# Weight blocks of a seven-product matrix multiplication: low parts by VectorE instead of by adding transfers, and four pieces of work moved in the order

## The chip, the cores and the metric

The kernel runs on one core of a Trainium2 chip. Times are device microseconds (us) of one execution; the time before is the median of three runs. The profile is of one further execution. TensorE (PE in the profile) multiplies, with its weight loads shown as PEld; VectorE is DVE, ScalarE ACT, GpSimd POOL, and SyncE (SP) only issues transfers. GpSimd issues transfers as well.

## The reference

One layer of a block: a short gated convolution, then a mixture of 16 experts of which each picks 256 of the 2048 tokens. All of it is in float32. What the change touches is the first product, `h @ w_in`, and the gates around the convolution:

```python
def dwconv_centred(x, w):                       # three taps along the tokens
    ...
def short_conv_mixer(h, w_in, conv_w, w_out):   # h: 2048 x 1024, w_in: 1024 x 3072
    gate_b, gate_c, v = jnp.split(h @ w_in, 3, axis=-1)
    return (gate_b * dwconv_centred(gate_c * v, conv_w)) @ w_out
    ...
m_l = (silu_c @ ada_w[i] + ada_b[i])[:, None, :]
sh1, sc1, g1, sh2, sc2, g2 = jnp.split(m_l, 6, axis=-1)
hl = modulate(rms_norm(lat, norm_g[i, 0]), sh1, sc1)
yl = short_conv_mixer(hl, sc_w_in[j], sc_conv[j], sc_w_out[j])
lat = lat + g1 * yl
hl2 = modulate(rms_norm(lat, norm_g[i, 1]), sh2, sc2)
lat = lat + g2 * expert_choice_ffn(hl2, moe_router[i], moe_w_gate[i], moe_w_up[i], moe_w_down[i])
```

## The kernel before, in words

**Split operands.** TensorE takes float32 operands in a rounded form, so every operand is held as a high part and a low part: ScalarE copies the value into the rounded form (high), VectorE subtracts that from the value (low). A product is three matmuls: high by high, low by high, high by low.

**Stages.** The 2048 tokens are four quarters of 512. Up to about 70 us the first quarter is normalised, turned and multiplied with two channel tiles of `w_in`; from 70 to 105 us the second quarter meets the same two tiles (`in_mm`, L507, called in the loop at L958 for `ct` 0 and 1, with eight pieces `k` each). From 105 to 592 us the other channel tiles follow, in **units** and **steps** (below). From 592 to 800 us comes `w_out` with the router, then a short search for the chosen tokens, and from about 840 us the experts.

**Units and steps.** A unit takes two tiles of 128 channels through 1024 tokens. Weights and tokens are each cut into 2 x 2 blocks, and the four results come out of seven block products where the plain way takes eight, with sums and differences of blocks as operands. There are 21 units: 20 of seven steps and one (unit 8, `PLAIN`) of eight plain steps, 148 steps in all. A step is twelve matmuls of 128x512 (`product`, L862). Units 0 to 8 work on the first half of the tokens, units 9 to 20 on the second.

**Weights.** A unit reads two pieces of `w_in`, `a` and `b`, of 512 KB, each in two halves. `make_block` (L829) makes the operand of one step. In its order 0 to 6 it takes half 0 of `a`; then `b0 + b1`, then that minus `a0`, both in place of `b0`; then half 1 of `a`; `b1 - b0` in place of `a0`; `a1 - b0` in place of `b0`; half 1 of `b`. VectorE makes these four sums (L840 to L846) at the start of the block that needs them, ScalarE copies the high part (L848). The low part is VectorE's subtraction (L855), but for blocks 0 and 6 (from unit 9 on also 3) it is a transfer: ScalarE writes the negated high part (L851) and GpSimd issues a transfer that reads the same weights from memory a second time and adds them on the way (L852). Three pieces have buffers; `piece_done` calls the load of the next one, on SyncE's queue.

**Order.** The order is written out by hand, engine by engine. At step n the program first makes the block of step n+3 (from unit 9 on, of step n+4), then what the table `later` holds for n, then the step's matmuls and the copy of its result. `at(n, f)` puts work into that table. Each engine runs its own list strictly in order.

**Banks.** A unit uses three banks of PSUM. Steps 0, 2, 4 and 6 add up in the first one, and ScalarE copies it out after each of them (L929), so step i+2 waits for the copy of step i. Steps 1 and 5 share the second, step 3 has the third; VectorE adds them to what was copied (L931 to L935).

**Behind a unit.** Two units of three hold `gate_c` and `v`. At the first step of the next unit VectorE multiplies them (L877) and ScalarE scales the result (L882); at the second step two more operations of VectorE (L886, L888) end the convolution. The third unit holds `gate_b`, with a product (L896) and a store.

**Operands made meanwhile.** The token sums of the first half are made by `first_sums` (L743) in the loop at L958, stored to memory and fetched again (`load_full`, `split_full`). Those of the second half are made in steps 4 to 41: the tokens are loaded (L408), normalised (`rstd_of` on ScalarE and GpSimd, then L417 on VectorE), turned by TensorE (L424) and stored, with sums (`save_sums`, `save_last`). From step 36 on, sums over `ada_w` (L562, L564) run on VectorE. Small tables are made in steps 4 to 43.

## Time and profile before

| | |
|---|---|
| median of three runs | 1920.81 us (1918.68 to 1926.13) |
| the profiled execution's own time | 1917.77 us |
| its span in the profile | 1916.0 us |
| TensorE busy | 1812.1 us, 95% of the span |
| VectorE busy | 1249.3 us, 65% |
| ScalarE busy | 951.2 us, 50% |
| GpSimd busy | 391.9 us, 20% |
| the steps (first matmul of L865 to the last) | 105.3 to 592.4 us |

A slice of the page's second part is 1916.0 / 40 = 47.9 us, so the steps lie in slices 3 to 13 of 40. The row PEclk gives the clock that TensorE was granted, in tenths; in the views by stretch it is a fraction. "[2.61 <-DMA sb" at the end of a row says that the engine was idle for 2.61 us and that the landing of a transfer into a tile named `sb` ended that. The tile `sb` is a block of weights, `raw` a piece of `w_in`, `tg` and `hl` are token operands, `pm` is a bank, `cx` and `cy` are the results of a unit, `xt` holds tokens and `pt` turned tokens, `aw` rows of `ada_w`, `fu` and `fy` fetched token sums.

### The profile page before, as it was taken

Reading aid. Unit: us, or ns where it says so; the run is one execution under the profiler, and the core shown is the slowest. Engines: PE = TensorE matmul, PEld = TensorE weight load, DVE = VectorE, ACT = ScalarE, POOL = GpSimd, SP = SyncE. Lnnn points to the kernel's source line nnn. Section 1 sums busy time; section 2 is a strip of 40 time slices with the busy share of each in tenths; the row PEclk is TensorE's granted clock in tenths of the full one; section 3 lists DMA queues with packets and bytes.
Section 4 is the critical chain, followed back from the end, with each engine's and each line's share of the span. In section 5 each row is a group of like instructions: output and inputs, shape, how many; then the busy total and the mean of one; then the engine's idle time right before and its main releaser. Section 6 shows DMA issues by size and latency. Waiting matters only on the chain.

```text
span 1916.0 us, 29497 instructions
## 1 busy us (share of the span) xinstructions
PE 1812.1 (95%) x11415; PEld 1600.4 (84%) x11415; DVE 1249.3 (65%) x1752; ACT 951.2 (50%) x1298; POOL 391.9 (20%) x552
## 2 busy tenths in 40 slices
PE   7977889999999999689999999999999999999997
PEld 6756667787788888479899999999999999999996
DVE  6554567666666667888667656665765666576653
ACT  5534434644444555557445444554545455445542
POOL 2223331233331222320021202102210211121002
PEclk9988999999999999889999999999999999999999
DMA  9474678777868899476687887878787878878774
GB/s 339 167 214 121 171 214 229 205 183 167 198 151 281 255 236 260 150 231 199 198 253 215 246 245 251 232 224 266 221 239 235 256 220 241 254 242 231 224 231 84
DMA packets 337229, 420.43 MB, mean 219 GB/s; under 512 B 104116, under 2 KB 201696, under 8 KB 337088
## 3 DMA queue, kind: packets, MB, share of 16 engines
q1 hardware_dynamic: 283632, 312.59, 53.4%
q0 software_dynamic: 53456, 105.96, 21.7%
q8 instruction: 89, 1.46, 0.3%
q14 instruction: 52, 0.43, 0.1%
HBM read 331.97 MB, written 63.98 MB: 207 GB/s over the span
## 4 chain that ended last, share of the span: by engine, by line
PE 71%; DVE 8%; DMA 7%; issue 6%; ACT 5%; POOL 2%; SPq 0%; POOLq 0%; DVEq 0%; ACTq 0%
PE pm L1587 12%; PE pm L1589 12%; PE pm L1591 11%; PE pm L1656 6%; PE pm L1654 6%; PE pm L1655 6%; PE pm L866 3%; PE pm L865 3%; PE pm L867 3%; DMA sb<-in_sc_w_in_dram 2%; PE pm L1116 2%; PE pm L1117 2%; PE pm L1119 2%; ACT sb L848 1%; DMA hl<-hl 1%
## 5 line engine op out<-in xcount | busy, mean ns | idle before, releaser
L248 DVE TENSOR_TENSOR ws<-raw,ws 128x1024 fp32r<-128x1024 f32 x390 | 463.5, 1221 | 272.7 <-ACT ws L238 272.7
L238 ACT ACTIVATE ws<-raw 128x1024 fp32r<-128x1024 f32 x390 | 394.2, 1052 | 408.9 <-PE pm L1591 325.0
L1587 PE MATMUL pm<-xT,ws 128*128 128x256 f32 x2048 | 568.3, 278 | 1.6 <-ACT xT L1566 1.6
L1589 PE MATMUL pm<-xT,ws 128*128 128x256 f32 x2048 | 567.0, 277 | 1.9 <-DVE xT L1567 1.8
L1591 PE MATMUL pm<-xT,ws 128*128 128x256 f32 x2048 | 566.6, 277 | 0.0
L1589 PEld LDWEIGHTS pm<-xT,ws 128*128 128x128 f32 x2048 | 385.4, 188 | 3.9 <-DVE xT L1567 2.1
L1587 PEld LDWEIGHTS pm<-xT,ws 128*128 128x128 f32 x2048 | 385.5, 188 | 3.2 <-ACT xT L1566 2.0
L1591 PEld LDWEIGHTS pm<-xT,ws 128*128 128x128 f32 x2048 | 385.3, 188 | 0.0
L1684 POOL DMA_INDIRECT out_dram<-ot,idx x30 | 104.9, 3498 | 587.3 <-DVE ot L1673 583.3
L865 PE MATMUL pm<-tg,sb 128*128 128x512 f32 x472 | 191.2, 405 | 13.4 <-ACT cx L929 11.8
L866 PE MATMUL pm<-tg,sb 128*128 128x512 f32 x472 | 189.4, 401 | 15.2 <-DMA sb<-in_sc_w_in_dram 14.9
L1656 PE MATMUL pm<-ws,hT 128*128 128x512 f32 x504 | 198.3, 394 | 0.0
L1654 PE MATMUL pm<-ws,hT 128*128 128x512 f32 x504 | 198.1, 393 | 0.0
L1655 PE MATMUL pm<-ws,hT 128*128 128x512 f32 x504 | 197.0, 391 | 0.0
L867 PE MATMUL pm<-tg,sb 128*128 128x512 f32 x472 | 187.9, 398 | 0.0
L848 ACT ACTIVATE sb<-raw 128x512 fp32r<-128x512 f32 x144 | 88.9, 625 | 125.9 <-DVE raw L840 47.2
L866 PEld LDWEIGHTS pm<-tg,sb 128*128 128x128 f32 x472 | 91.4, 194 | 38.5 <-DMA sb<-in_sc_w_in_dram 18.7
L855 DVE TENSOR_TENSOR sb<-raw,sb 128x512 fp32r<-128x512 f32 x92 | 63.6, 692 | 91.1 <-ACT sb L848 91.1
L865 PEld LDWEIGHTS pm<-tg,sb 128*128 128x128 f32 x472 | 91.2, 193 | 38.0 <-ACT cx L929 16.4
L1656 PEld LDWEIGHTS pm<-ws,hT 128*128 128x128 f32 x504 | 94.7, 188 | 20.0
L1655 PEld LDWEIGHTS pm<-ws,hT 128*128 128x128 f32 x504 | 94.7, 188 | 19.8
L1654 PEld LDWEIGHTS pm<-ws,hT 128*128 128x128 f32 x504 | 94.7, 188 | 18.7
(388 smaller groups left out, 2743.5 us busy)
## 6 DMA issues: line engine op xcount, KB each, us to landing
raw<-in_moe_w_down_dram SPq DMA_DIRECT2D x128, 512.0 KB, 4.6
raw<-in_moe_w_gate_dram SPq DMA_DIRECT2D x126, 512.0 KB, 4.8
raw<-in_moe_w_up_dram SPq DMA_DIRECT2D x126, 512.0 KB, 4.3
raw<-in_sc_w_in_dram SPq DMA_DIRECT2D x42, 512.0 KB, 4.8
xt<-in_x_dram SPq DMA_DIRECT2D x32, 512.0 KB, 7.6
aw<-in_ada_w_dram POOLq DMA_DIRECT2D x32, 512.0 KB, 5.1
sb<-in_sc_w_in_dram POOLq DMA_DIRECT2D x52, 256.0 KB, 5.4
fu<-fscr SPq DMA_DIRECT2D x23, 512.0 KB, 4.4
```

What stands on the lines that cost most here:

```text
L238: nc.scalar.activation(t[:, 0], raws[n_high], AF.Copy)
L248: (eng or nc.vector).tensor_sub(t[:, 1, ..., s], raw[..., s], t[:, 0, ..., s].bitcast(F32))
L848: nc.scalar.activation(t[:, 0], full, AF.Copy)
L865: nc.tensor.matmul(o, t[:, 0, j], r[:, 0], start=(first and j == 0), stop=False, skip_group_check=True)
L866: nc.tensor.matmul(o, t[:, 1, j], r[:, 0], start=False, stop=False, skip_group_check=True)
L867: nc.tensor.matmul(o, t[:, 0, j], r[:, 1], start=False, stop=end, skip_group_check=True)
L1587: nc.tensor.matmul(o, w[:, 0, j, c0], xT[:, 0, k], start=(k == 0 and f % 2 == 0), stop=False, skip_group_check=True)
L1589: nc.tensor.matmul(o, w[:, 0, j, c0], xT[:, 1, k], start=False, stop=False, skip_group_check=True)
L1591: nc.tensor.matmul(o, w[:, 1, j, c0], xT[:, 0, k], start=False, stop=(k == KD - 1), skip_group_check=True)
L1654: nc.tensor.matmul(ps[s], h, w[:, 0, j], start=(k == 0), stop=False)
L1655: nc.tensor.matmul(ps[s], h, w[:, 1, j], start=False, stop=False)
L1656: nc.tensor.matmul(ps[s], l, w[:, 0, j], start=False, stop=(k == KD - 1))
```

## The change

1. Every low part of a weight block is VectorE's subtraction. L851 and L852 are gone.
2. Each of the four weight sums is made at the end of the block before the one that uses it. The load after piece `a` is called at the end of block 4 instead of block 5.
3. VectorE's additions from the banks after steps 3, 4 and 5 stand in the list of the next step.
4. In the loop at L958, `load_other` and `first_sums` come three or four pieces earlier, so that all four are in the first of the two tiles; the split of the first token sum is a function of its own, and the fetches are called earlier.
5. The roots (`rstd_of`) of the third and fourth quarter stand two steps ahead of the normalisation that uses them. For the third quarter the roots are at steps 6 to 9 (with the normalisation at 7 to 10 before, now 8 to 11) and the turns at 13 to 16 (11 to 14 before); for the fourth the loads are at step 16 (15), the roots at 18 to 21 (18 to 21), the normalisation at 20 to 23 (18 to 21).
6. The turns of the fourth quarter (`save_other`) stand a step ahead of the sums that use them: turns at 24, 28, 32, 36 (23, 27, 31, 35), sums at 25, 29, 33, 37 (23, 27, 31, 35), the last difference at 27, 31, 35, 39 (25, 29, 33, 37).
7. One buffer of 4 KB goes from the tiles `wide` (six to five) to the tiles `hl` (18 to 19); of the output stage's token tiles every third is now one of the latter.

VectorE, blocks 0 to 4 of the first unit (the loop's last pieces and step 0), before:

```order
L797 TENSOR_TENSOR tg<-fu,tg 128x2x512 x2
L840 TENSOR_TENSOR raw<-raw 128x512
L855 TENSOR_TENSOR sb<-raw,sb 128x512
L797 TENSOR_TENSOR tg<-fu,tg 128x2x512
L842 TENSOR_TENSOR raw<-raw 128x512
L855 TENSOR_TENSOR sb<-raw,sb 128x512 x2
```

And in the changed kernel, where L849 is the low part, L855 to L861 are the four sums and L807 is the split of fetched token sums:

```order
L807 TENSOR_TENSOR tg<-fu,tg 128x2x512
L849 TENSOR_TENSOR sb<-raw,sb 128x512
L855 TENSOR_TENSOR raw<-raw 128x512
L807 TENSOR_TENSOR tg<-fu,tg 128x2x512
L849 TENSOR_TENSOR sb<-raw,sb 128x512
L857 TENSOR_TENSOR raw<-raw 128x512
L807 TENSOR_TENSOR tg<-fu,tg 128x2x512
L849 TENSOR_TENSOR sb<-raw,sb 128x512 x2
L859 TENSOR_TENSOR raw<-raw 128x512
```

Block 0 has a subtraction of its own now, and each sum stands behind a low part instead of ahead of one.

VectorE, the last two steps of unit 10 and the first two of unit 11, before (L935 is a bank addition, L877 the product of `gate_c` and `v`):

```order
L855 TENSOR_TENSOR sb<-raw,sb 128x512
L564 SCALAR_TENSOR_TENSOR acc<-aw,s_col,acc 128x1024
L935 TENSOR_TENSOR cx<-cx,pm 128x512
L844 TENSOR_TENSOR raw<-raw 128x512
L855 TENSOR_TENSOR sb<-raw,sb 128x512
L877 TENSOR_TENSOR cy<-cx,cy 128x1024
L846 TENSOR_TENSOR raw<-raw 128x512
L855 TENSOR_TENSOR sb<-raw,sb 128x512
```

The same place now (L881 is the product):

```order
L849 TENSOR_TENSOR sb<-raw,sb 128x512
L564 SCALAR_TENSOR_TENSOR acc<-aw,s_col,acc 128x1024
L935 TENSOR_TENSOR cy<-cy 128x512
L849 TENSOR_TENSOR sb<-raw,sb 128x512
L859 TENSOR_TENSOR raw<-raw 128x512
L935 TENSOR_TENSOR cx<-cx,pm 128x512
L849 TENSOR_TENSOR sb<-raw,sb 128x512
L861 TENSOR_TENSOR raw<-raw 128x512
L881 TENSOR_TENSOR cy<-cx,cy 128x1024
L849 TENSOR_TENSOR sb<-raw,sb 128x512
```

The bank addition (`cx<-cx,pm`) has moved behind the next step's low part, which is VectorE's now, and a weight sum (L861) stands between the last low part and the product.

ScalarE around steps 7 and 8, where the first convolution starts, before (L287 is the square of a root, L882 the scaling, L848 a high part):

```order
L848 ACTIVATE sb<-raw 128x512
L287 ACTIVATE junk,ss<-xt 128x1024
L882 ACTIVATE cx<-cy,v_col 128x1024
L929 ACTIVATE cx<-pm 128x512
L848 ACTIVATE sb<-raw 128x512
L287 ACTIVATE junk,ss<-xt 128x1024
```

And now (L886 is the scaling, L933 the copy of a bank):

```order
L287 ACTIVATE junk,ss<-xt 128x1024
L933 ACTIVATE cy<-pm 128x512
L848 ACTIVATE sb<-raw 128x512
L287 ACTIVATE junk,ss<-xt 128x1024
L886 ACTIVATE cx<-cy,v_col 128x1024
L933 ACTIVATE cx<-pm 128x512
```

The squares begin a step earlier; the one of step 7 still stands ahead of the scaling.

The diff, cut to its core:

```diff
@@ first_sums
-            t = wide("tsum", [P, 2, QT])
+            t = tsum[j] = wide("tsum", [P, 2, QT])
             nc.vector.tensor_sub(t[:, 0], f[:, 0], lo[:, 0])
-            t1 = home(0, T1, j)
-            nc.scalar.activation(t1[:, 0], t[:, 0], AF.Copy)
             nc.vector.tensor_sub(t[:, 1], f[:, 1], t[:, 0])
...
-            nc.vector.tensor_sub(t1[:, 1], t[:, 0], t1[:, 0].bitcast(F32))
...
+        def first_split(j):
+            t, t1 = tsum.pop(j), home(0, T1, j)
+            nc.scalar.activation(t1[:, 0], t[:, 0], AF.Copy)
+            nc.vector.tensor_sub(t1[:, 1], t[:, 0], t1[:, 0].bitcast(F32))
...
+        def rstd_to(q, b):
+            rstds[q, b] = rstd_of(xq[q][b], hl_tile([P, D], BF, "junk"))
...
+        def save_other(j):
             hi = hi_of[j] = hl_tile([P, 2, QT], F32, "fx")
             for h in range(2):
                 turn_x(3, j + 4 * h)
                 full_x(3, j + 4 * h, hi[:, h])
@@ make_block
-            if u != PLAIN:
-                if i == 1:
-                    nc.vector.tensor_add(full, full, raw_half(b, 1))
-                elif i == 2:
-                    nc.vector.tensor_sub(full, full, raw_half(a, 0))
-                elif i == 4:
-                    nc.vector.tensor_sub(full, raw_half(b, 1), raw_half(b, 0))
-                elif i == 5:
-                    nc.vector.tensor_sub(full, raw_half(a, 1), full)
-                    piece_done(a)
             nc.scalar.activation(t[:, 0], full, AF.Copy)
-            if u != PLAIN and i in ((0, 6) if u < PLAIN else (0, 3, 6)):
-                src, offset, ap, _ = pieces[p]
-                nc.scalar.activation(t[:, 1], t[:, 0].bitcast(F32), AF.Copy, scale=-1.0)
-                nc.gpsimd.dma_start(t[:, 1], dram(src, offset + h * (KD // 2) * ap[1][0], [ap[0], [ap[1][0], KD // 2], ap[2]]),
-                                    accum_op=ALU.add)
-            else:
-                nc.vector.tensor_sub(t[:, 1], full, t[:, 0].bitcast(F32))
+            nc.vector.tensor_sub(t[:, 1], full, t[:, 0].bitcast(F32))
...
+            if i == 0:
+                nc.vector.tensor_add(raw_half(b, 0), raw_half(b, 0), raw_half(b, 1))
+            elif i == 1:
+                nc.vector.tensor_sub(raw_half(b, 0), raw_half(b, 0), raw_half(a, 0))
+            elif i == 3:
+                nc.vector.tensor_sub(raw_half(a, 0), raw_half(b, 1), raw_half(b, 0))
+            elif i == 4:
+                nc.vector.tensor_sub(raw_half(b, 0), raw_half(a, 1), raw_half(b, 0))
+                piece_done(a)
@@ unit_step
-            if i == 3:
-                nc.vector.tensor_add(x[:, q0], x[:, q0], o)
-            elif i == 4:
-                nc.vector.tensor_add(y[:, q1], y[:, q1], y[:, q0])
-            elif i == 5:
-                nc.vector.tensor_add(x[:, q1], x[:, q1], o)
+            if i in (3, 4, 5):
+                at(n + 1, lambda: nc.vector.tensor_add(*((x[:, q0], x[:, q0], o), (y[:, q1], y[:, q1], y[:, q0]),
+                                                         (x[:, q1], x[:, q1], o))[i - 3]))
@@ the loop over k, first tile (ct == 0)
+                    if k < 2:
+                        load_other(0, k)
+                    if k in (2, 4, 5, 6):
+                        j = (2, 4, 5, 6).index(k)
                         first_sums(j)
...
@@ the table
-            at(7 + n, lambda b=n: norm_x(2, b, None, rstd_of(xq[2][b], hl_tile([P, D], BF, "junk"))))
-            at(11 + n, lambda j=n: save_full(j))
-            at(15, lambda b=n: load_x(3, b, b + 1))
-            at(18 + n, lambda b=n: norm_x(3, b, None, rstd_of(xq[3][b], hl_tile([P, D], BF, "junk"))))
-            at(21 + 4 * n, lambda j=n: load_other(1, j))
-            at(23 + 4 * n, lambda j=n: save_sums(j))
-            at(25 + 4 * n, lambda j=n: save_last(j))
+            at(6 + n, lambda b=n: rstd_to(2, b))
+            at(8 + n, lambda b=n: norm_x(2, b, None, rstds.pop((2, b))))
+            at(13 + n, lambda j=n: save_full(j))
+            at(16, lambda b=n: load_x(3, b, b + 1))
+            at(18 + n, lambda b=n: rstd_to(3, b))
+            at(20 + n, lambda b=n: norm_x(3, b, None, rstds.pop((3, b))))
+            at(22 + 4 * n, lambda j=n: load_other(1, j))
+            at(24 + 4 * n, lambda j=n: save_other(j))
+            at(25 + 4 * n, lambda j=n: save_sums(j))
+            at(27 + 4 * n, lambda j=n: save_last(j))
```

More of the change, by code (lines that the diff above doesn't have):

```diff
@@ L374, in hl_tile @@
         def hl_tile(shape, dt=F32R, name="hl"):
-            return mix.tile(shape, dt, name=name, tag="hl", bufs=18)
+            return mix.tile(shape, dt, name=name, tag="hl", bufs=19)
         def big_tile(shape, dt=F32R, name="ws"):
@@ L383, in wide @@
         def wide(name, shape=[P, 2 * QT + 4], dt=F32):
-            return cvp.tile(shape, dt, name=name, tag="wide", bufs=6)
+            return cvp.tile(shape, dt, name=name, tag="wide", bufs=5)
         def m2(name, n=QT, dt=F32):
@@ L766, in save_sums @@
                 full_x(3, j + 4 * h, hi[:, h])
+        def save_sums(j):
+            lo = lo_of[j] = rows_F.pop(j)
+            hi = hi_of[j]
             nc.gpsimd.dma_start(fscr[1][B22, j], hi[:, 1])
@@ L858, in make_block @@
                     piece_done(p)
+                return
+            if i == 0:
[7 more added lines that the diff above has]
+                piece_done(a)
             elif i == 6:
@@ L1091, in m2 @@
             return mixd.tile([P, n], dt, name=name, tag="m2", bufs=5)
+        n_xt = [0]
         def b4(name, shape=[P, D]):
-            if name == "xt":
-                return mixd.tile(shape, F32, name=name, tag="xt", bufs=3)
+            n_xt[0] += name == "xt"
+            if name == "xt" and n_xt[0] % 3:
+                return mixd.tile(shape, F32, name=name, tag="xt", bufs=2)
             return hl_tile(shape, F32, name)
```

34 lines of the change are left out of this document (15 added, 19 removed).

## The prediction, made before the change was run

> **What bounds the kernel now.** I read the page's slices first, then stretches along the steps, then TensorE's waits there.
>
> ```profile
> PE   7977889999999999689999999999999999999997
> PEclk9988999999999999889999999999999999999999
> ```
>
> TensorE is full except in the first six slices and around slice 17, the search, which the change does not touch. So the first third of the steps is where time can be had. The stretches are steps 0-20, 21-41, 42-55, 56-147, and steps 95-110 as a measure.
>
> ```profile
> core 0: us, PE busy (x) PEld busy (x) DVE busy (x) ACT busy (x) POOL busy (x), PEclk, DMA share, GB/s
> 105.30:202.10 96.80, 72.92 (x285) 56.62 (x284) 46.99 (x74) 43.23 (x70) 27.15 (x107) 0.86 0.54 148
> 202.10:285.70 83.60, 69.32 (x286) 54.60 (x285) 52.63 (x73) 34.53 (x59) 28.45 (x46) 0.92 0.69 201
> 285.70:329.70 44.00, 41.08 (x173) 31.95 (x172) 34.62 (x44) 21.32 (x35) 8.15 (x12) 1.00 0.75 208
> 329.70:592.40 262.70, 257.62 (x1118) 209.06 (x1117) 177.10 (x220) 131.60 (x215) 75.08 (x101) 1.00 0.78 192
> 442.90:486.40 43.50, 43.50 (x193) 36.03 (x192) 29.98 (x37) 21.04 (x35) 14.61 (x19) 1.00 0.77 181
> ```
>
> The measure: 16 steps in 43.5 us, 2.72 us each, at full clock. 148 steps make 402.6 us. The steps also hold eight groups of turns and eight sums of `ada_w`:
>
> ```profile
> 181.00 1.03 PE L424 MATMUL pt<-identf,xt 128*128 128x128 f32 x8
> L571 PE MATMUL pt<-acc,ones_f 128*128 128x512 f32 x16 | 7.6, 596 | 0.3 <-DVE acc L564 0.3
> ```
>
> At about 0.9 (the 1.03 overlaps its neighbour) and 7.6 in all, that is 7.2 + 7.6, and the floor is 417.4 us. The stage takes 592.4 - 105.3 = 487.1. The excess of 69.7 is waits, and matmuls at half clock.
>
> ```profile
> PE pm L866 <- DMA sb<-in_sc_w_in_dram: 21.1, 12, 4.8
> PE pm L865 <- ACT cx L929: 11.8, 7, 2.6
> PE pt L424 <- DVE xt L417: 11.0, 4, 4.1
> PE pm L865 <- ACT sb L848: 1.4, 1, 1.4
> ```
>
> These make 45.3 us (total, times, longest). Half clock costs 0.14 x 96.8 + 0.08 x 83.6 = 20.2. The remaining 4 are shorter waits and restarts. The first wait, in the timeline (start, duration, engine), shows all of it:
>
> ```profile
> 103.24 1.37 POOL L852 DMA_DIRECT2D sb<-in_sc_w_in_dram  x1 [0.55 <-ACT sb L851]
> 105.28 0.39 PE L865 MATMUL pm<-hl,sb 128*128 128x512 f32 x1
> 108.28 0.80 PE L866 MATMUL pm<-hl,sb 128*128 128x512 f32 x1 [2.61 <-DMA sb<-in_sc_w_in_dram]
> 108.87 0.63 PE L867 MATMUL pm<-hl,sb 128*128 128x512 f32 x1
> ```
>
> The transfer, issued at 103.24, lands 5 us later; TensorE idles 2.61 us and then takes 0.63 for a matmul instead of 0.39.
>
> The Trainium skill, "TensorE: Matmul & The Clock Gate", section "Part 1: The HAM clock gate (the "warmup" mystery)", halves the clock after an idle window of about 3.4 us. The trace differs: 2.61 was enough. By the rule the slow clock that I leave below (3.4 us) would be nothing and the time 1874; the row decides.
>
> **Low parts by VectorE.** Per block it removes 0.63 us of ScalarE, 1.37 of GpSimd and a landing, and adds one L855 to VectorE (groups by line: count, busy time, mean ns, idle time before):
>
> ```profile
> L851 ACT ACTIVATE sb<-sb 128x512 fp32r<-128x512 f32 x51 | 32.3, 633 | 1.6
> L852 POOL DMA_DIRECT2D sb<-in_sc_w_in_dram x51 | 67.9, 1367 | 127.3 <-ACT sb L851 126.2 <-issue 0.8
> L855 DVE TENSOR_TENSOR sb<-raw,sb 128x512 fp32r<-128x512 f32 x92 | 63.6, 692 | 91.1 <-ACT sb L848 91.1
> ```
>
> Steps 0-20 and 21-41 have six such blocks each, steps 42-55 four, the rest 36. VectorE's busy time becomes 47.0 + 4.2 = 51.2, 52.6 + 4.2 = 56.8, 34.6 + 2.8 = 37.4 and 177.1 + 24.9 = 202.0. The floors of these stretches are 60.7 (21 x 2.72 + 3.6), 60.7, 39.1 and 256. So it hides, but VectorE is at 94 and 96% in the second and third. The 21.1 us go whole.
>
> **Weight sums a block ahead.** No work is added. ScalarE's high part no longer waits for VectorE:
>
> ```profile
> L848 ACT ACTIVATE sb<-raw 128x512 fp32r<-128x512 f32 x143 | 88.3, 625 | 125.9 <-DVE raw L840 47.2 <-DVE raw L842 35.0 <-DVE raw L846 28.8
> L840 DVE TENSOR_TENSOR raw<-raw 128x512 f32<-128x512 f32 x20 | 13.7, 685 | 1.0 <-DMA raw<-in_sc_w_in_dram 1.0
> ```
>
> That ends the 1.4 and the stalls of ScalarE behind which copies of banks were late. But it lengthens one chain. At a unit's first step VectorE's product and ScalarE's scaling stand ahead of the copy for which TensorE waits two steps on; unit 11 started at 393.5 (timeline):
>
> ```profile
> 393.70 0.60 ACT L929 ACTIVATE cy<-pm 128x512 f32<-128x512 f32 x1 [1.67 <-PE pm L867]
> 394.19 0.62 ACT L848 ACTIVATE sb<-raw 128x512 fp32r<-128x512 f32 x1
> 394.85 0.69 DVE L855 TENSOR_TENSOR sb<-raw,sb 128x512 fp32r<-128x512 f32 x1 [0.88 <-ACT sb L848]
> 395.46 1.22 DVE L877 TENSOR_TENSOR cy<-cx,cy 128x1024 f32<-128x1024 f32 x1
> 396.79 1.16 ACT L882 ACTIVATE cx<-cy,v_col 128x1025 f32<-128x1025 f32 x1 [1.98 <-DVE cy L877]
> 397.86 0.57 ACT L929 ACTIVATE cx<-pm 128x512 f32<-128x512 f32 x1
> 398.94 0.39 PE L865 MATMUL pm<-tg,sb 128*128 128x512 f32 x1
> ```
>
> The copy ended at 398.43, 0.5 ahead of its user at 398.94. A sum of 0.685 now stands between L855 and L877, so TensorE waits 0.2 at each of 14 units: **2.8 us**. Where VectorE comes late to that place, the lateness is added.
>
> ```profile
> L768 DVE TENSOR_TENSOR fy<-fx,fy 128x512 f32<-128x512 f32 x4 | 2.8, 693 | 6.9 <-ACT fx L715 6.9
> L888 DVE SCALAR_TENSOR_TENSOR cx<-cy,v_col,cx 128x1025 f32<-128x1025 f32 (+1 forms) x14 | 18.0, 1286 | 1.1
> L564 DVE SCALAR_TENSOR_TENSOR acc<-aw,s_col,acc 128x1024 f32<-128x1024 f32 x28 | 35.8, 1278 | 6.0 <-DMA aw<-in_ada_w_dram 6.0
> ```
>
> I keep a running balance of VectorE's list per step against 2.72 us, never under zero, in durations of these rows (L768 stands for a token sum or a bank addition, two L888 for the end of a convolution) and of L840, L855 and L877. Step 25 has a low part, a weight sum, a bank addition and four token sums, 4.8 us; step 29 is 6.7 (a low part, a weight sum, 2.57 and four token sums); 37 to 43 average 3.2 with an L564 in most. The balance is 0.6 at step 28, 1.9 at 35 and 3.0 at 49: **5.5 us**. It falls to zero between bursts from unit 9 on, except where an L564 meets the product (steps 92, 120, 134). There waits of 1.1 and 0.6 stand among the 11.8 now; each of three grows by 0.7: **3.7 us**.
>
> The balance peaks at 6.8, at step 43. A block has three steps, 8.2 us, less about 2 for copy, high and low part, so it comes 0.6 late there; L564's 6.0 us for its `aw` fall into the same stretch, and the bound is 0.6 to 6.6. I take **4 us**.
>
> **Bank additions a step back.** VectorE no longer waits for the end of the current step. The price is ScalarE's copy of step 6, which overwrites what step 4's addition reads; that addition ends 3.3 us after the start of step 5, 2.1 before the copy, so it costs nothing while the balance is under 2.1. At the peak it is in the 4 us.
>
> **Roots and turns.** The turns of step 11 waited for a chain of square, root and normalisation inside one step (timeline; the last row is a load's time to landing):
>
> ```profile
> 163.52 0.48 PE L424 MATMUL pt<-identf,xt 128*128 128x128 f32 x1 [4.14 <-DVE xt L417]
> 168.08 1.33 PE L424 MATMUL pt<-identf,xt 128*128 128x128 f32 x5 [4.08 <-DVE xt L417]
> 167.27 0.75 DVE L417 TENSOR_SCALAR xt<-xt,rstd 128x1024 f32<-128x1024 f32 x1 [3.81 <-POOL rstd L290]
> xt<-in_x_dram SPq DMA_DIRECT2D x8, 512.0 KB, 7.6
> ```
>
> Now two steps lie between, and the 8.2 us of the third quarter go. Its squares begin at step 6, after loads called at step 4 that take 7.6 to land: ScalarE stands about 2 us, and the scaling of step 7 has a square ahead of it: **2 us** at step 9. For the fourth quarter the last normalisation is one step ahead of the turn: it ends about 3.6 us after step 23 starts, against 2.72: **0.9 us**, where 2.8 stood.
>
> **Token sums of the first half.** They move into the first tile's 19 us (70 to 89), where VectorE has to do 20 us of work; it ends about 7 late, inside the second tile's 16 us. TensorE had no wait there. Their fetches are called 6 to 10 us sooner; one held ScalarE for 7.2 us in step 0, behind which the 1.4 and two L929 waits stand:
>
> ```profile
> L796 ACT ACTIVATE tg<-fu 128x1024 fp32r<-128x1024 f32 x15 | 15.7, 1045 | 7.2 <-DMA fu<-fscr 7.2
> ```
>
> I cost the move at nothing; without that cover block 0 is late, by up to 3 us.
>
> **Buffers.** Five `wide` tiles are as many as a group of three units holds, so the copy of a fourth unit's second result can wait for a product (L896, 1.2 us) with a step of 2.72 in between: nothing. The output stage had waits of under 2 us in 200 and keeps its three token tiles: nothing.
>
> **The sum.** After: 2.8 + 5.5 + 3.7 + 4 + 2 + 0.9 = 18.9 us of waits. Slow clock: I allow two windows of half clock, 3.4 us lost (the 2.61 us wait above cost some 2). Restarts and late landings that I can't see: 4, as now. Excess 26.3, stage 443.7, gain 69.7 - 26.3 = 43.4. The profiled execution's own time, 1917.8, becomes 1874.4. The median of the runs is 3.0 above that execution, so the forecast is **1877 us**.
>
> **Rivals.**
> - *VectorE becomes the bound*, in lockstep with ScalarE. For: 94 and 96% above, and L855 waits 0.99 us per block (91.1 / 92). If that is not hidden in steps 0-55, they take 51.2 + 56.8 + 37.4 + 56 x 0.99 = 200.8 against 224.4 now; with 1.5 from later steps the gain is 25: 1896. Against: a wait of VectorE is spare time while it is ahead, and goes when it is behind.
> - *Almost everything goes*: an excess of 8 us, 1859. For: the balance counts no slack in ScalarE. Against: L564 and its `aw`.
> - *Locked port.* GpSimd's copy ahead of L882 takes 0.63 us for two elements:
>
> ```profile
> L878 POOL COPY cy<-carry 128x2 f32<-128x2 f32 x14 | 8.7, 625 | 0.0
> ```
>
>   If VectorE's two-input work holds it up by one instruction more at 14 units, 9.7 us: 1887. The row alone speaks for it. The Trainium skill, "SBUF — State Buffer", section "SBUF: two separate sides", states such a lock between a VectorE operation with two SBUF inputs and a GpSimd one that reads SBUF; no run here shows it apart.
> - *Slower.* VectorE falls over 2.7 us behind at each unit's start, so each of 20 units loses the longest L929 wait, 2.6, and a half-clock window, 1.7: 86 us against 65.5 recovered (45.3 + 20.2): 1941. Against: 79% load from step 56 on.
> - *No change.* Pieces of weights, called 8.2 us before use, land in over 10 us, and some 30 of them are 2.2 late: 66 us, 1921. Against: L840 waited 1.0 us for `raw` in all.
>
> **Numbers.** Forecast 0.52 (own range 1865 to 1890), lockstep 0.20, almost everything 0.12, port 0.06, slower 0.05, no change 0.05. A measurement tells 0.5%, about 10 us, from no change. Faster 0.90, same 0.05, slower 0.05. The range of 1857 to 1901 holds the forecast, the port, most of lockstep, and the nearer part of almost everything.
>
> **What would show it.** Right: no wait of TensorE on a transfer in the steps; the clock at 0.97 or more from 105 to 300; L424's wait under 3 us; steps 0-55 in 175 to 190 us; a wait of 0.2 on L929 at most units. Wrong: VectorE near 100% in steps 21-55 with TensorE waiting for low parts (lockstep); GpSimd as ScalarE's releaser at the scaling (port); waits on `raw` (no change).

## The result, and the profile after

The changed kernel takes 1868.93 us (median of four runs, 1868.14 to 1870.37) against 1923.47 us of the kernel before (four runs, 1918.68 to 1927.15): a ratio of 0.9719, with a 95% interval of 0.9692 to 0.9745. The forecast was 1877 us with a range of 1857 to 1901. The profiled execution took 1868.36 us with a span of 1866.3, against 1917.8 and 1916.0 before.

First the page's slices of the kernel after:

```profile
PE   7999989999999999599999999999999999999997
PEclk9999999999999999799999999999999999999999
```

Slices 3 to 6 of TensorE's row, which stood at 7, 7, 8 and 8, are now 9, 9, 9 and 8, and the clock, at 8 in slices 3 and 4 before, stays at 9 up to the search. The stretches of the steps, in the columns of the same view of before (the whole stage, then steps 0-20, 21-41, 42-55 and 56-147):

```profile
105.24:543.20 437.96, 425.34 (x1858) 344.79 (x1857) 334.92 (x457) 194.23 (x323) 80.78 (x215) 0.99 0.54 172
105.24:168.60 63.36, 61.20 (x285) 50.52 (x284) 46.06 (x77) 38.15 (x64) 26.93 (x103) 1.00 0.52 175
168.60:231.30 62.70, 61.31 (x286) 50.55 (x285) 50.90 (x73) 28.77 (x49) 18.91 (x37) 1.00 0.65 216
231.30:280.20 48.90, 43.45 (x174) 33.46 (x173) 38.85 (x52) 19.85 (x32) 6.29 (x10) 0.93 0.61 200
280.20:543.20 263.00, 259.37 (x1118) 210.26 (x1117) 199.11 (x258) 107.45 (x179) 28.65 (x65) 0.99 0.50 156
```

The stage fell from 487.1 to 438.0 us: 49.1 of the span's 49.7 us are here. Over the floor of 417.4 us it has an excess of 20.6, where 69.7 stood and 26.3 was forecast. VectorE is busy in 73, 81, 79 and 76% of the four stretches. What TensorE still waits for in the stage (total, times, longest):

```profile
PE pm L869 <- ACT cx L933: 8.1, 5, 2.3
PE pt L571 <- DVE acc L564: 4.0, 1, 4.0
PE pt L424 <- DVE xt L417: 0.4, 1, 0.4
```

No wait on a transfer is left (21.1 us before), and the waits on the normalised tokens fell from 11.0 to 0.4. The longest wait is new, at the sum of `ada_w` for the searched router, before step 47. Two groups by line show the two halves of a block now (count, busy, mean ns, idle before):

```profile
L849 DVE TENSOR_TENSOR sb<-raw,sb 128x512 fp32r<-128x512 f32 x144 | 98.5, 688 | 85.8 <-ACT sb L848 85.4
L848 ACT ACTIVATE sb<-raw 128x512 fp32r<-128x512 f32 x144 | 88.6, 626 | 53.8 <-DVE raw L855 23.5
```

VectorE forms all 144 low parts, at 688 ns. ScalarE's idle time ahead of the high parts went from 125.9 to 53.8 us.

### The profile page after: what moved, and what is told of

Its sections match the earlier page's. It is cut to its first block, busy times and chain, and to the rows that moved or that the text cites. A ratio compares the mean times of both kernels' runs of the same rounds, so it can differ in the third digit from the quotient of the medians.

```text
span 1866.3 us, 29372 instructions
## 1 busy us (share of the span) xinstructions
PE 1798.3 (96%) x11415; PEld 1595.0 (85%) x11415; DVE 1276.3 (68%) x1804; ACT 916.9 (49%) x1246; POOL 333.1 (18%) x500
## 4 chain that ended last, share of the span: by engine, by line
PE 82%; DVE 6%; DMA 4%; issue 4%; ACT 3%; POOL 1%; POOLq 0%; SPq 0%; ACTq 0%; DVEq 0%
PE pm L1595 12%; PE pm L1597 12%; PE pm L1599 12%; PE pm L1664 6%; PE pm L1662 6%; PE pm L1663 6%; PE pm L869 5%; PE pm L870 5%; PE pm L871 5%; PE pm L1124 2%; PE pm L1125 2%; PE pm L1127 2%; DMA hl<-hl 1%; PE pm L511 1%; PE pm L512 1%
## 5 line engine op out<-in xcount | busy, mean ns | idle before, releaser
L869 PE MATMUL pm<-tg,sb 128*128 128x512 f32 x472 | 187.2, 397 | 8.2 <-ACT cx L933 8.1
L871 PE MATMUL pm<-tg,sb 128*128 128x512 f32 x472 | 184.6, 391 | 0.0
L870 PE MATMUL pm<-tg,sb 128*128 128x512 f32 x472 | 184.5, 391 | 0.0
L849 DVE TENSOR_TENSOR sb<-raw,sb 128x512 fp32r<-128x512 f32 x144 | 98.5, 688 | 85.8 <-ACT sb L848 85.4
L869 PEld LDWEIGHTS pm<-tg,sb 128*128 128x128 f32 x472 | 89.0, 189 | 31.5 <-ACT cx L933 13.0
L848 ACT ACTIVATE sb<-raw 128x512 fp32r<-128x512 f32 x144 | 88.6, 626 | 53.8 <-DVE raw L855 23.5
L871 PEld LDWEIGHTS pm<-tg,sb 128*128 128x128 f32 x472 | 89.0, 189 | 18.9
```

The lines of the kernel that those rows point to most:

```text
L869: nc.tensor.matmul(o, t[:, 0, j], r[:, 0], start=(first and j == 0), stop=False, skip_group_check=True)
L870: nc.tensor.matmul(o, t[:, 1, j], r[:, 0], start=False, stop=False, skip_group_check=True)
L871: nc.tensor.matmul(o, t[:, 0, j], r[:, 1], start=False, stop=end, skip_group_check=True)
```

## The experiments

Twelve kernels were run beside the kernel before. Five of them (u) undo one part of the change, three (o) make one part alone in the kernel before, four (n) change the result further. "Stage" is the time of the 148 steps in the profiled execution, from one row of the view by stretches each; the rest of the span lay between 1423 and 1433 us in all fourteen kernels, so the stage holds the larger differences. Each ratio is to runs of the kernel before in the same session, with medians of 1920.1 to 1923.5 us. Executions of one kernel spread by 2 to 16 us, and the stage is that of a single one: for n2 and o3 it comes from the slowest.

| kernel | median us | ratio to before, 95% interval | stage us |
|---|---|---|---|
| before | 1923.5 | 1 | 487.1 |
| after | 1868.9 | 0.9719 (0.9692 to 0.9745) | 438.0 |
| u1 adding transfers back | 1900.8 | 0.9893 (0.985 to 0.9937) | 473.6 |
| u2 weight sums back | 1880.7 | 0.9787 (0.9741 to 0.9832) | 449.4 |
| u3 bank additions back | 1870.9 | 0.9731 (0.9689 to 0.9773) | 436.4 |
| u4 roots and turns back | 1878.1 | 0.9765 (0.9722 to 0.9808) | 449.6 |
| u5 token sums back | 1877.3 | 0.9770 (0.9752 to 0.9789) | 448.2 |
| o1 low parts alone | 1896.7 | 0.9856 (0.984 to 0.9873) | 467.4 |
| o2 weight sums alone | 1907.6 | 0.9924 (0.99 to 0.9949) | 477.3 |
| o3 roots and turns alone | 1912.6 | 0.9952 (0.9935 to 0.9969) | 486.0 |
| n1 sum of `ada_w` later | 1862.9 | 0.9683 (0.9667 to 0.9699) | 434.0 |
| n2 and product first | 1858.6 | 0.9659 (0.9643 to 0.9675) | 430.5 |
| n3 and carry by VectorE | 1863.8 | 0.9694 (0.9678 to 0.971) | 430.9 |
| n4 product first where it pays | 1855.0 | 0.9650 (0.963 to 0.9671) | 423.8 |

### u1: adding transfers back

```diff
-            nc.vector.tensor_sub(t[:, 1], full, t[:, 0].bitcast(F32))
+            if u != PLAIN and i in ((0, 6) if u < PLAIN else (0, 3, 6)):
+                nc.scalar.activation(t[:, 1], t[:, 0].bitcast(F32), AF.Copy, scale=-1.0)
+                nc.gpsimd.dma_start(t[:, 1], dram(...), accum_op=ALU.add)
+            else:
+                nc.vector.tensor_sub(t[:, 1], full, t[:, 0].bitcast(F32))
```

> The changed kernel with the adding transfers back in blocks 0 and 6 of a unit (0, 3 and 6 from unit 9 on), all else as changed (1868.9 us). Theory (the transfers were late by themselves, 21.1 us of TensorE waits and most of the 20.2 us of half clock before): 1888 to 1910 us, TensorE's waits on sb from DRAM back at 12 to 24 us in the steps, and half-clock slices beside them. Rival (they were late because ScalarE's list stood behind VectorE's weight sums, which now run ahead): under 1876 us, waits on sb under 5 us.

1900.8 us, 31.9 more than the changed kernel. TensorE's waits:

```profile
PE pm L876 <- DMA sb<-in_sc_w_in_dram: 27.0, 12, 4.8
PE pm L875 <- ACT cx L939: 7.6, 6, 1.9
PE pt L571 <- DVE acc L564: 1.4, 1, 1.4
```

The transfers are late although ScalarE hardly stands for weight sums any more: its idle time for them ahead of high parts is 20.4 us here against 122.1 in the kernel before. Their lateness is their own, as the theory had it; the rival falls. From issue to landing they took 6.0 us in the median and up to 10.7. The stage is 35.6 us longer; TensorE's waits make 23.5 of that (36.0 in these rows against 12.5). The remaining 12 are longer matmuls: TensorE is busy for 437.4 us against 425.3, and the granted clock is 0.68 to 0.82 in steps 0, 6, 20, 41 and 55. The wait at L571 is 1.4 instead of 4.0, with 51 subtractions fewer on VectorE.

### u2: weight sums back in front of their own block

```diff
+            if u != PLAIN:
+                if i == 1:
+                    nc.vector.tensor_add(full, full, raw_half(b, 1))
+                ...
             nc.scalar.activation(t[:, 0], full, AF.Copy)
             nc.vector.tensor_sub(t[:, 1], full, t[:, 0].bitcast(F32))
-            if i == 0:
-                nc.vector.tensor_add(raw_half(b, 0), raw_half(b, 0), raw_half(b, 1))
-            ...
```

> The changed kernel with each weight sum back in front of its own block's high part. Theory (ScalarE then stands behind VectorE, and the copies of banks behind ScalarE): waits of TensorE on L933's copies grow by 6 to 13 us and the steps' time by 8 to 18: 1877 to 1887 us. Rival (the time was all in the transfers, the order of the sums is worth nothing): 1867 to 1872 us.

1880.7 us, 11.8 more, inside the theory's range.

```profile
PE pm L870 <- ACT cx L934: 14.1, 11, 4.3
PE pt L424 <- DVE xt L417: 3.3, 1, 3.3
```

The waits on copies of banks are 14.1 us in 11 places against 8.1 in 5: ScalarE stands behind VectorE's sums (103.2 us of idle time ahead of high parts against 45.1), and the copies behind ScalarE. The wait on a turn grew too, from 0.4 to 3.3, while the one at L571 (4.0) is gone. Slower matmuls make another 5.0 us (TensorE busy for 430.4 us against 425.3).

### u3: bank additions back in their own step

```diff
-            if i in (3, 4, 5):
-                at(n + 1, lambda: nc.vector.tensor_add(...))
+            if i == 3:
+                nc.vector.tensor_add(x[:, q0], x[:, q0], o)
+            elif i == 4:
+                nc.vector.tensor_add(y[:, q1], y[:, q1], y[:, q0])
+            elif i == 5:
+                nc.vector.tensor_add(x[:, q1], x[:, q1], o)
```

> The changed kernel with the bank additions back in the step whose matmuls they follow. Theory (the additions make VectorE stand at the end of a step with the low parts and weight sums behind them; a block has three steps to spare): 0 to 6 us more, 1869 to 1875 us, with VectorE's wait on PE up and the low parts still ahead of their users. Rival (VectorE's list is what the first 56 steps hang on, so an in-order wait there goes straight into the end): 1880 us or more, with TensorE's waits on low parts or on the sum of ada_w up.

1870.9 us, 1.9 more, with an interval that overlaps the changed kernel's; its stage is 1.6 us shorter. Its longest wait is L571's, 3.9 us, as in the changed kernel. The rival falls: VectorE has enough spare time to stand at the end of a step.

### u4: roots, turns and saves by the old table

```diff
-            at(6 + n, lambda b=n: rstd_to(2, b))
-            at(8 + n, lambda b=n: norm_x(2, b, None, rstds.pop((2, b))))
-            at(13 + n, lambda j=n: save_full(j))
+            at(7 + n, lambda b=n: rstd_to(2, b))
+            at(7 + n, lambda b=n: norm_x(2, b, None, rstds.pop((2, b))))
+            at(11 + n, lambda j=n: save_full(j))
...
```

> The changed kernel with the old table for the loads, roots, turns and saves of the third and fourth quarters. Theory (11.0 us of waits on xt came from root and turn in one step, against 2.4 us left now, and each wait of over 2 us brings 1 to 2 us of half clock): 1878 to 1888 us, waits of L424 and its step back at 8 to 11 us. Rival (the root waits came from ScalarE's list, held up by the transfers and sums that are gone): 1868 to 1873 us, waits on xt under 4 us.

1878.1 us, 9.2 more: the size that the theory gave. The form is another.

```profile
PE pm L869 <- ACT cx L933: 13.0, 6, 3.1
PE pt L424 <- DVE xt L417: 4.6, 2, 3.1
```

Only 4.6 us are waits on the tokens, not 8 to 11; another 4.9 us came as waits on copies of banks (13.0 against 8.1), which stand on the same ScalarE list as the squares. Part of what stood as waits on turns before was owed to other parts; o2 below shows which.

### u5: token sums of the first half back

```diff
-                    if k < 2:
-                        load_other(0, k)
-                    if k in (2, 4, 5, 6):
-                        first_sums((2, 4, 5, 6).index(k))
-                    ...
+                    if k in (5, 7):
+                        first_sums((k - 5) // 2)
+                    ...
                 else:
+                    if k in (0, 2):
+                        first_sums(2 + k // 2)
+                    if k == 3:
+                        load_full(1)
+                        load_full(3)
```

> The changed kernel with the token sums of the first half and their fetches back in their old places. Theory (costed at nothing, hidden under the first two tiles): within 2 us of the changed kernel, 1867 to 1871 us. Rival (their fetches then land late again, hold ScalarE some 7 us at the start of the steps, and the first blocks are late): 1872 to 1877 us, with TensorE waits in steps 0 to 4.

1877.3 us, 8.3 more. The rival is right, 0.3 us above its range. The edit also puts the first weight block and one load of weights a piece of the loop later, where they stood before; it is the rows that tie the time to the fetches. ScalarE's timeline around the start of the steps, and after it TensorE's:

```profile
108.55 1.06 ACT L804 ACTIVATE tg<-fu 128x1024 fp32r<-128x1024 f32 x1 [6.56 <-DMA fu<-fscr]
109.51 0.61 ACT L846 ACTIVATE sb<-raw 128x512 fp32r<-128x512 f32 x1
```

```profile
110.18 0.50 PE L867 MATMUL pm<-tg,sb 128*128 128x512 f32 x1 [1.49 <-ACT sb L846]
...
117.08 0.80 PE L867 MATMUL pm<-tg,sb 128*128 128x512 f32 x1 [2.77 <-ACT cx L931]
```

ScalarE stands 6.56 us for a group of token sums that was written to DRAM and fetched back too late. The high part behind it is late, and then a copy; the last matmul shown takes 0.80 us at half clock. Steps 0 to 2 take 15.7 us instead of 8.2, which is 7.5 of the 10.2 us by which the stage is longer.

### o1, o2, o3: one part alone in the kernel before

o1 makes every low part with VectorE:

```diff
-            if u != PLAIN and i in ((0, 6) if u < PLAIN else (0, 3, 6)):
-                ...
-                nc.gpsimd.dma_start(t[:, 1], dram(...), accum_op=ALU.add)
-            else:
-                nc.vector.tensor_sub(t[:, 1], full, t[:, 0].bitcast(F32))
+            nc.vector.tensor_sub(t[:, 1], full, t[:, 0].bitcast(F32))
```

> The kernel before with one part of the change: VectorE subtracts all low parts; sums, bank additions, roots and turns, token sums and buffers as before. Theory (the parts are worth about the same in either kernel; the transfers cost 31.9 us in the changed one): 32 us under before, 1884 to 1894 us. Rival (without the earlier sums and bank additions VectorE's list, now longer, holds ScalarE up, and a part of the gain shows as waits on copies of banks): 1896 to 1910 us, waits on L929's copies above the 11.8 us of before.

26.7 us under before, just inside the rival's range.

```profile
PE pm L859 <- ACT cx L923: 19.7, 12, 3.7
PE pt L424 <- DVE xt L417: 7.3, 3, 3.0
PE pm L859 <- ACT sb L848: 5.3, 2, 4.4
```

The transfers' waits are gone, but the waits on copies are 19.7 us in 12 places against 11.8 in 7, and those on high parts 5.3 against 1.4. So the rival's mechanism is there: without the other parts some 5 of the 32 us are waited for elsewhere.

o2 puts the weight sums a block ahead in the kernel before, with the adding transfers left in place; its edit is u2's diff read backwards:

```diff
-            if u != PLAIN:
-                if i == 1:
-                    nc.vector.tensor_add(full, full, raw_half(b, 1))
-                ...
+            if i == 0:
+                nc.vector.tensor_add(raw_half(b, 0), raw_half(b, 0), raw_half(b, 1))
+            ...
```

> The kernel before with only the weight sums a block ahead; adding transfers, bank additions, roots, turns and token sums as before. Theory (ScalarE standing behind the sums makes the waits on copies of banks, 11.8 us, whatever the transfers do): 8 to 14 us under before, waits on copies under 8 us, waits on sb from DRAM still 18 to 28 us. Rival (each part needs the others: with the transfers in place the time saved is waited for at the next transfer): within 4 us of before.

12.6 us under before, as in u2 to within a microsecond. The rows only half support the reason given:

```profile
PE pm L866 <- DMA sb<-in_sc_w_in_dram: 15.9, 8, 4.3
PE pm L865 <- ACT cx L929: 13.1, 7, 2.8
```

The waits on copies did not fall (13.1 against 11.8). What fell are the waits on transfers, from 21.1 to 15.9, below the expected 18, and those on turns, from 11.0 to 4.2; the one at L571 grew from 0.3 to 2.4.

o3 uses the new table for roots, turns and saves:

```diff
-            at(7 + n, lambda b=n: norm_x(2, b, None, rstd_of(xq[2][b], ...)))
-            at(11 + n, lambda j=n: save_full(j))
+            at(6 + n, lambda b=n: rstd_to(2, b))
+            at(8 + n, lambda b=n: norm_x(2, b, None, rstds.pop((2, b))))
+            at(13 + n, lambda j=n: save_full(j))
...
```

> The kernel before with only the new table for loads, roots, turns and saves of the third and fourth quarters. Theory (worth the same as in the changed kernel, 9.2 us): 6 to 14 us under before, waits on xt under 3 us. Rival (the waits on xt move to the adding transfers next to them): within 4 us of before, waits on sb from DRAM above 24 us.

7.5 us under before in the median; its profiled stage is only 1.1 shorter. In that execution the waits on turns fell from 11.0 to 1.8 us, and those on transfers, copies and high parts grew to 24.6, 16.5 and 3.7, by 3.5, 4.7 and 2.3, which is the rival's mechanism. That execution, of 1917.7 us, was the slowest of six (1907.6 to 1917.7), so its rows may overstate what the others lost.

**What follows from the eight.** Undone one by one the five parts cost 31.9, 11.8, 1.9, 9.2 and 8.3 us, 63.1 together, more than the 54.5 of the whole. Low parts alone give 26.7 where their removal costs 31.9, and roots and turns 7.5 against 9.2. TensorE waits for whichever of several lists is last, so a part that takes away one wait lets another appear; the parts are worth most together. Weight sums are the exception, with 12.6 alone against 11.8. By far the largest is the adding transfer.

### n1: the sum of `ada_w` two steps later

The new wait of 4.0 us at L571 was the place to gain next. Timeline of the changed kernel there:

```profile
241.07 0.55 POOL L905 DMA_DIRECT2D vscr<-cx  x1 [3.60 <-DVE cx L900]
241.61 0.41 POOL L906 COPY carry<-cx 128x1 f32<-128x1 f32 x1
241.96 0.54 POOL L551 DMA_DIRECT2D aw<-in_ada_w_dram  x1
...
249.35 1.29 DVE L564 SCALAR_TENSOR_TENSOR acc<-aw,s_col,acc 128x1024 f32<-128x1024 f32 x1 [1.44 <-DMA aw<-in_ada_w_dram]
...
250.78 1.19 PE L571 MATMUL pt<-acc,ones_f 128*128 128x512 f32 x1 [4.03 <-DVE acc L564]
```

The last slice of `ada_w` is issued at 241.96, behind a save that GpSimd held until VectorE's gate product was done. It then took 7.3 us to land, where the five before it took 4.1 to 6.0 (those with a landing on record; the transfers moved 289 GB/s from 242 to 249 us, against 172 over the stage). VectorE is idle for 1.44 us before the slice can be added, and TensorE for 4.03.

```diff
-            at(47, lambda s=n: load_full(6 + s))
+            at(47 if n < 3 else 50, lambda s=n: load_full(6 + s))
...
-            at(36 + t * 5 // 4, lambda t=t: ada_step(5, t))
+            at(36 + t * 5 // 4 if t <= KD else 49, lambda t=t: ada_step(5, t))
```

> The changed kernel with the sum over partitions of the searched router's ada_w rows (L571, L572) at step 49 instead of 47, and the last of the four loads that then wait for its tile at step 50 instead of 47. Theory (4.0 us of wait on acc and the half clock around it, 10 us in all in steps 45 to 47, come from VectorE's addition being late there): 6 to 10 us under the changed kernel, 1859 to 1863 us, no wait at L571 and the clock near 1 from 240 to 260 us. Rival (VectorE is behind at that place whatever waits on it, so the next user, a low part or a copy, takes the wait over): 1867 to 1870 us.

1862.9 us, 6.0 under the changed kernel: the theory, with the smallest gain that it allowed. No wait at L571 is left, and no other user took it over; a new wait of 0.8 us on a copy at step 50 took a little back. The profiled stage is only 4.0 us shorter, in part because half clock fell on step 9 there (4.14 us instead of 2.85).

### n2, n3: product first, and GpSimd's small copies

n2 (on top of n1):

```diff
-                at(n + 1, lambda: conv_start(ps_, ct, x, y))
+                later.setdefault(n + 1, []).insert(0, lambda: conv_start(ps_, ct, x, y))
...
             if i == 0:
                 st = {}
+            if n >= n1:
+                for f in later.pop(n, []):
+                    f()
```

> n1, and from step 71 on the product, the scaling and the other deferred work of a step stand ahead of its block, the product first of all. Theory (the weight sum and the additions for ada_w ahead of the product make the 2.3 and 1.2 us waits and the pairs of 0.2 at a unit's third step): 4 to 7 us under n1, waits on L933 after step 71 under 1 us in all. Rival (VectorE then stands for the copy that the product reads and low parts come late): no change or slower than n1, with waits on sb in place of those on L933.

In the code `n1` is step 64: from there on all deferred work stands ahead of the step's block. Before it only `conv_start` moves, to the front of the deferred work.

1858.6 us, 4.3 under n1. From step 71 on every step takes 2.72 us, apart from those that hold a sum of `ada_w`, so the order of the lists was the cause there. It was not VectorE's list alone: `conv_start` also holds the scaling and two small operations of GpSimd, and the largest wait that went, at step 94, had come from GpSimd (see "An addition for `ada_w` meets the product" below). Before step 56 the new order cost time: a turn at step 14 waited 2.0 us, and steps 29, 33 and 43 took 0.6 to 1.1 us more than 2.72.

n3 (on top of n2) moves three small copies from GpSimd:

```diff
-            nc.gpsimd.tensor_copy(v[:, 0:2], carry[:, ct, 0:2])
+            nc.vector.tensor_copy(v[:, 0:2], carry[:, ct, 0:2])
...
-                nc.gpsimd.tensor_copy(carry[:, ct, 0:2], v[:, n:n + 2])
+                nc.vector.tensor_copy(carry[:, ct, 0:2], v[:, n:n + 2])
...
-                nc.gpsimd.tensor_copy(carry[:, ct, 2:3], gate[:, n + 1:n + 2])
+                nc.vector.tensor_copy(carry[:, ct, 2:3], gate[:, n + 1:n + 2])
```

> n2, with the three small copies of carried columns (two elements ahead of the scaling, two after the convolution, one after the gate) on VectorE instead of GpSimd. Theory (before steps 37 and 46 ScalarE stood 3.2 and 2.9 us for such a copy, because GpSimd's list stood behind its DMA issues): the waits of 1.0 and 1.4 us there go, 1 to 4 us under n2. Rival (the price of more instructions on VectorE, or nothing): within 1 us of n2 or slower.

1863.8 us, and a stage of 430.9 against 430.5: no gain. The waits on copies ahead of steps 37 and 46 (1.4 and 1.2 us, 1.3 and 1.6 in n2) stayed, so GpSimd was not what TensorE hung on there. The median is 5.2 us above n2's while the profiled stages agree, because n2's profile is of its slowest execution, 1864.0 us of 1856.0 to 1864.0. By the medians the move cost some 5 us; why is not shown.

### n4: product first where it pays

```diff
-                later.setdefault(n + 1, []).insert(0, lambda: conv_start(ps_, ct, x, y))
+                if n + 1 in (14, 28, 35):
+                    at(n + 1, lambda: conv_start(ps_, ct, x, y))
+                else:
+                    later.setdefault(n + 1, []).insert(0, lambda: conv_start(ps_, ct, x, y))
```

> n2, but the product of the units that end at steps 13, 27 and 34 stays behind the other deferred work, as in n1. Theory (in n2 the product stood in VectorE's list ahead of work on which the turns of step 14 and copies at steps 29, 33 and 43 hang; 7 us of steps were lost there, and the clean steps from 71 on stay): 4 to 8 us under n2's 1858.6, 1851 to 1855 us. Rival (these losses come from VectorE's total work before step 56, not from its order): 1856 to 1860 us.

1855.0 us (1851.2 to 1855.7), 3.6 under n2 where 4 to 8 were expected; the stage is 6.7 us shorter, more than the medians differ, since n2's is that of its slowest execution. Steps 14, 29, 33 and 43 are back at the lengths that they have in the changed kernel. Its interval of the ratio lies under that of the changed kernel. The stage, in the columns of the view by stretches:

```profile
105.18:528.95 423.77, 418.88 (x1858) 342.78 (x1857) 334.93 (x457) 194.76 (x322) 81.69 (x215) 1.00 0.56 178
```

TensorE's largest waits are four on copies of banks, 4.0 us in all. VectorE does the same 334.9 us of work as in the changed kernel in a stage that is 14.2 us shorter and 6.4 over the floor. So its total load was not the limit; the order of the lists was.

## Why the prediction was right, and where it was not

The forecast was 8 us high. The profiled execution came out at 1868.4 us against 1874.4, of which 5.7 lie in the steps (438.0 against 443.7). The rest comes from the 3.0 that was added for the median of the runs: the changed kernel's median lies only 0.6 above its profiled execution. The main mechanism held: the transfers' waits went whole and the subtractions that took their place hid. Several smaller terms came out near their size for other reasons than those given, and that part is luck.

| term of the sum | forecast | measured |
|---|---|---|
| product chain, 14 x 0.2 | 2.8 | 1.8, at 5 units |
| VectorE late at steps 30, 37, 51 | 5.5 | 1.0, at step 37 alone |
| an addition for `ada_w` meets the product | 3.7 | 3.5: 1.2 at step 122, and 2.3 at step 94 by another cause |
| balance peak, steps 37 to 47 | 4 | 5.4: 4.0, and 1.4 that belongs to the buffers |
| step 9 | 2 | 2.2, by another cause |
| turn of step 24 | 0.9 | 0.4 |
| half clock | 3.4 | 5.1 |
| restarts and the rest | 4 | 1.2, what is left |
| excess | 26.3 | 20.6 |

- **Low parts by VectorE.** Right: "the 21.1 us go whole", and u1 brings 27.0 us of transfer waits back. The subtractions hide.
- **Weight sums.** The mechanism holds in u2 (14.1 us of waits on copies), the price was never split off; it is 11.8. With the transfers still there (o2) the same edit paid through other waits.
- **VectorE late at steps 30, 37 and 51.** What failed here is the running balance, which charged each instruction the mean duration of its row. Timeline of the changed kernel, VectorE without a pause:

```profile
240.69 0.68 DVE L849 TENSOR_TENSOR sb<-raw,sb 128x512 fp32r<-128x512 f32 x1
241.29 0.68 DVE L861 TENSOR_TENSOR raw<-raw 128x512 f32<-128x512 f32 x1
241.89 1.28 DVE L564 SCALAR_TENSOR_TENSOR acc<-aw,s_col,acc 128x1024 f32<-128x1024 f32 x1
243.09 1.22 DVE L900 TENSOR_TENSOR cx<-cx,cy 128x1023 f32<-128x1023 f32 x1
```

  The starts are 0.60, 0.60 and 1.20 us apart, each 0.08 less than the duration. Back to back an instruction costs 0.08 less than its row says, some 0.3 us for a step of four. By that estimate a burst of ten steps makes 3 of the 4.5 us that were forecast in excess; no run tests it apart. In steps 0-55 the durations of VectorE's 202 rows add up to 147.0 us and its busy time, which counts overlapping time once, to 135.8 (46.06 + 50.90 + 38.85). The 145.4 that were forecast as busy time had 207 instructions, so only a part of that difference is overlap. The row quoted in the prediction showed it already (a low part of 0.69 at 394.85, the product at 395.46).
- **An addition for `ada_w` meets the product.** At step 122 it does. At step 94 the product was done at 384.62, and the scaling began 2.28 us later, for GpSimd's small operations; these stood behind a load of `ada_w` that waited for another transfer to land. Timeline of the changed kernel:

```profile
383.40 1.22 DVE L881 TENSOR_TENSOR cy<-cx,cy 128x1024 f32<-128x1024 f32 x1
386.11 0.56 POOL L551 DMA_DIRECT2D aw<-in_ada_w_dram  x1 [2.47 <-DMA rows<-dst]
386.90 1.15 ACT L886 ACTIVATE cx<-cy,v_col 128x1025 f32<-128x1025 f32 x1 [6.60 <-POOL cy L884]
388.58 0.50 PE L869 MATMUL pm<-tg,sb 128*128 128x512 f32 x1 [2.28 <-ACT cx L933]
```

  The 2.28 us are TensorE's wait, and a stretch of half clock follows. So this price lay in GpSimd's list, which the prediction did not follow; the kernel before had it too (1.72 us behind the product, and TensorE's 1.1).
- **Step 9.** The size is luck. The prediction gave it to ScalarE, held by the third quarter's loads and squares. Timeline of the changed kernel:

```profile
127.79 0.15 DVE L121 TENSOR_SCALAR rep_i<-rep_i 128x1 int32<-128x1 int32 x1 [0.82 <-POOL rep_i L120]
129.03 1.22 DVE L881 TENSOR_TENSOR cy<-cx,cy 128x1024 f32<-128x1024 f32 x1
130.36 1.15 ACT L886 ACTIVATE cx<-cy,v_col 128x1024 f32<-128x1024 f32 x1 [3.67 <-DVE cy L881]
```

  ScalarE stood idle for 3.67 us until VectorE's product was done, and the product stood behind small tables (L121 to L130) that waited for GpSimd. The kernel before had 2.6 us of TensorE's waits at this place, behind the same product. In n4, with the product ahead of the tables, the scaling begins at 128.16, a square does stand between it and the copy, and TensorE's wait is 1.1 us.
- **The balance peak.** The late `ada_w` was seen, and 4 us were the right size for it, but its victim was not a block: it was the sum over `ada_w` itself, and the half clock behind it came on top. n1 shows it: moving that sum alone gives 6.0 us.
- **Half clock.** Two windows were allowed and two came, around step 46 and in step 94, but they cost some 3.4 and 1.7 us (an estimate: 13.0 us from 243.7 on at a granted 0.74 and 9.6 from 383.4 on at 0.82, so 13.0 x 0.26 and 9.6 x 0.18).
- **Bank additions at nothing.** Right (u3).
- **Roots and turns.** "The 8.2 us of the third quarter go": u4 measures 9.2, half of it through copies of banks.
- **Token sums at nothing.** Wrong: 8.3 us (u5). The step named the ScalarE wait of 7.2 us, and the waits behind it, and then credited their end to the weight sums; it looked for TensorE's waits in the tiles where the sums stand, not where their fetches land. The total did not suffer, since the excess was taken off by its symptoms and this part was in the change as well; that is luck.
- **Buffers at nothing.** Not quite. Timeline of the changed kernel, behind the rows of L905 and L906 that stand under n1:

```profile
242.05 0.60 ACT L933 ACTIVATE cy<-pm 128x512 f32<-128x512 f32 x1 [2.95 <-POOL carry L906]
...
243.71 0.50 PE L869 MATMUL pm<-tg,sb 128*128 128x512 f32 x1 [1.38 <-ACT cx L933]
```

  A copy waited 2.95 us for a `wide` tile, and TensorE 1.38 behind it. In n3, where VectorE makes the small copy, the same copy of a bank still waits 1.82 us, so it hangs on the gate product's tile and not on GpSimd. A run with six tiles was not made.
- **The rivals.** Lockstep falls: VectorE is at 73 to 81%, and n4 does the same work 14 us faster. The locked port falls as a cost at the scaling: GpSimd's copy there took 289 ns in the mean (L882, 14 times) against 625, and n3 gains nothing. Its sign did come, GpSimd as ScalarE's releaser at four of 14 scalings (five before), and cost time at step 94; but there the copy itself took 0.20 us, and GpSimd's order made it late. "Almost everything goes" did not happen, but its 8 us of excess is nearly what n4 reaches (6.4). No wait on `raw` appeared.
- **What would show it.** Of the five signs of the forecast three came: no transfer waits, L424 at 0.4, steps 0-55 in 175.0 us, the lower edge of what was given. The clock fell to 0.93 in steps 42-55, and the wait of 0.2 came at 5 units, not most.

## What to carry to other kernels

A short transfer that adds into a tile which the matmuls need soon costs more than its waits: here 27 us of waits were 32 us of time, and a subtraction on an engine with a fifth of its time free removed them. When several in-order lists feed one engine, follow each of them, an almost idle one too; cost a moved piece at what it stands in front of, its fetches included, and look for the wait where those land; waits credited to one cause move to the next when it alone is removed. Keep a balance of an engine's list by the distance between starts, not by the durations of the rows.

## What the hardware showed that was not expected

**Half clock does not follow from the length of one wait.** In u1 a wait of 1.95 us is followed, 0.6 us after TensorE restarts, by 3.4 us of matmuls at 0.63 (until 425.41, where one takes 0.45 again); in u4 a wait of 2.74 us is followed by none. So not every wait of over 2 us brings half clock, as the expectation for u4 had it. Timeline of u1, then of u4:

```profile
421.49 0.50 PE L875 MATMUL pm<-tg,sb 128*128 128x512 f32 x1 [1.95 <-ACT cx L939]
422.05 0.57 PE L877 MATMUL pm<-tg,sb 128*128 128x512 f32 x1
422.42 0.63 PE L875 MATMUL pm<-tg,sb 128*128 128x512 f32 x1
```

```profile
132.67 0.50 PE L869 MATMUL pm<-tg,sb 128*128 128x512 f32 x1 [2.74 <-ACT cx L933]
133.01 0.39 PE L870 MATMUL pm<-tg,sb 128*128 128x512 f32 x1
```

The same place shows it too: ahead of step 9 TensorE waited 2.16 us in the changed kernel, in n1 and in u5, and 2.17 in u3. Step 9 then took 2.85 us at full clock in the changed kernel and in u3, but 4.14 at a granted 0.67 in n1 and 4.44 at 0.62 in u5.

The Trainium skill, "TensorE: Matmul & The Clock Gate", section "Part 1: The HAM clock gate (the "warmup" mystery)", has a free-running window of about 3.4 us; the length of the slow stretch agrees with it, and a free-running window would explain why equal waits differ and why the shorter one can be the dearer. That a whole window must be idle does not agree: 1.95 us of waiting was enough. No run here varied the phase, so that reading is an argument and not shown.

**A one-column copy on GpSimd took 2.81 us**, and ended when VectorE paused. Timeline of the changed kernel:

```profile
244.82 1.28 DVE L564 SCALAR_TENSOR_TENSOR acc<-aw,s_col,acc 128x1024 f32<-128x1024 f32 x1
245.14 2.81 POOL L906 COPY carry<-cy 128x1 f32<-128x1 f32 x1
246.02 1.28 DVE L849 TENSOR_TENSOR sb<-raw,sb 128x512 fp32r<-128x512 f32 x2
247.22 0.68 DVE L855 TENSOR_TENSOR raw<-raw 128x512 f32<-128x512 f32 x1
```

VectorE's four instructions follow without a pause to 247.90, and the copy ends at 247.95. The rule of the locked port that the prediction weighed (the Trainium skill, "SBUF — State Buffer", section "SBUF: two separate sides") fits this one row. No wait of TensorE hung on it: the next one, at 250.78, was for VectorE's sum over `ada_w`.
